# The context vector's adaLN products of a two-layer hybrid transformer, made by VectorE alone

## The chip, the cores and the metric

The kernel runs on one core of a Trainium2 chip. The metric is device time in microseconds (us), the median of the runs shown. The engines are TensorE (PE; its weight loads are PEld), VectorE (DVE), ScalarE (ACT), GpSimd (POOL) and SyncE (SP), which issues most loads. Each takes its own queue of instructions in order.

## The reference

Two layers work on a latent stream of 512 tokens and a context stream of 256 tokens, 1024 features each. Every sub-layer is normalised and modulated by shift, scale and gate vectors that come from a conditioning vector, one for the latent stream (`c`) and one for the context stream (`c_ctx`):

```python
silu_c = jax.nn.silu(c)
silu_cc = jax.nn.silu(c_ctx)
for layer in range(DEPTH):
    mod_l = (silu_c @ w_mod[layer] + b_mod[layer]).reshape(b, N_SUB, 3, 1, D_MODEL)
    mod_c = (silu_cc @ w_mod[layer] + b_mod[layer]).reshape(N_SUB, 3, D_MODEL)
    xl = macaron_ffn(xl, norm_g[layer, 0], mod_l[:, 0, 0], mod_l[:, 0, 1], mod_l[:, 0, 2], ...)
    xc = macaron_ffn(xc, norm_g[layer, 0], mod_c[0, 0], mod_c[0, 1], mod_c[0, 2], ...)
    # then a mixer (neighbourhood attention and Fourier mixing, or grouped attention
    # and spatial gating), and a second feed-forward with sub-layer 2's vectors
def modulate(h, shift, scale):
    return h * (1 + scale) + shift
def macaron_ffn(x, g, shift, scale, gate, w_gu, w_down):
    h = modulate(rms_norm(x, g), shift, scale)
    return x + 0.5 * gate * swiglu(h, w_gu, w_down)
```

`w_mod` is 1024 by 9216 for each layer. The last sub-layers need no context vectors, because only the latent stream is returned.

## The kernel before

Activations lie feature-major on the chip, eight tiles of 128 features by 768 tokens. Every float32 operand of a product is split in two float32r parts, high and low, and three products (L303 to L305) make one. The high part is a cast on ACT, the low part a subtraction on DVE (`fill`, L324 and L325, for weights; `finish`, L414 and L415, for activations).

The products with `w_mod` are not made by PE. A row block of 128 outputs by 512 or 1024 inputs is loaded with one output per partition, multiplied by silu(c) or silu(c_ctx), which lies repeated on every partition, and summed along the row. `mod_row` does this for each of the vectors in `vecs`: vector 0 is the latent one, vector 1 the context one. `mod_finish` adds the bias and prepares scale and gate.

Where the rows are made:

- `start_up` makes the vectors of the first sub-layer, rows of 1024, 24 of them for both vectors, k tile by k tile, between the first loads, the first norm and the first block products. `two_rows` gives each pair of rows one of three places in turn.
- `mod_jobs` makes jobs of half a row block, 512 columns. In `ffn`, `tick` adds a share to a counter after each group of products, and each time that it passes one, a job is traced. The first feed-forward has 96 jobs for both vectors, the second 80 for both, the third 64 for the latent vector alone, the fourth none. A job's weights go to `wm`, which has two buffers, by a load on SP's queue (L183); silu of the second half of the features replaces the first half's midway.

The order on the engines is set by a planner that simulates the program's times, within the dependencies. Besides those, `issue_after(ins)` puts what is traced inside behind `ins` on the engine of `ins`. `dve_last` is the newest of the DVE instructions that the block products wait for, and jobs pass it as `behind`. `pool_last` is the last POOL sum of `combos`, which makes four sums of blocks of the input.

Around the jobs, `gu_w` makes a tile of gate and up products by seven block products: seven weight blocks are formed by four POOL sums (L516 to L522) and split by ACT and DVE, ACT copies the first two results out of PSUM (L541, L544), DVE makes the sums of the others (L547, L551, L554, L555, L560), and ACT and DVE form the activations (L549 to L561). PE may write on in a bank only when ACT's copy of it is done.

Of the kernel before, what the change touches and what calls it, by code (L numbers as in the profile page):

```python
# [15 lines left out]
ALU = mybir.AluOpType  # L16
# [37 lines left out]
def hybrid_backbone_kernel(ctx: ExitStack, tc: tile.TileContext, A: dict, out: bass.AP):  # L54
# [9 lines left out]
    def opened(name, **kw):  # L64
        """a pool that is open from here until its second part is called"""
        es = ExitStack()
        return es.enter_context(tc.tile_pool(name=name, bufs=1, reuse_waits="tile", **kw)), es.close

    # PSUM: four banks, and four more that are single or in pairs as the phase wants them
# [20 lines left out]
    # ---------------------------------------------------------------- constants  # L90
# [13 lines left out]
    def load_constants(pool, l, shape):  # L104
        """per-head gains (those of the queries with the scores' factor, negated), head selectors and their transposes"""
        name = ("ab", "cd")[l]
        g = pool.tile([P, 2], F32, name="gq")
        nc.sync.dma_start(g, A["gqk_" + name])
        V.tensor_scalar(g[:, 0:1], g[:, 0:1], -HD ** -0.5, None, ALU.mult)
        res = [g]  # L110
        for a, sh in (("sel_", [P] + shape), ("bsel_", [32 + shape[1], shape[0], P])):
            o = pool.tile(sh, F32R, name=a + name)
            nc.gpsimd.dma_start(o, A[a + name])
            res.append(o)
        return res
# [4 lines left out]
    # ---------------------------------------------------------------- work that is emitted between groups of products  # L120
    pending = []
    down_last, act_last, pool_last = [], [], []
# [13 lines left out]
    # ---------------------------------------------------------------- adaLN vectors  # L136
    def load_silc(tiles, d0, n):
        """silu(c) and silu(c_ctx), n elements from d0, on every partition"""
        for v, t in enumerate(tiles):
            nc.sync.dma_start(t, A["cb"][:, v, d0:d0 + n])  # L140
            ACT.activation(t, t, AF.Silu)
        return tiles

    def mod_row(w, junk, silc, vecs, outs, behind=()):
        """products of 128 rows of weights with silc, an element of the vector per partition"""
        for v in vecs:
            if v == 1:
                with issue_after(pool_last):
                    POOL.tensor_tensor(w, w, silc[v], op=ALU.mult)  # L149
                ACT.activation(w, w, AF.Copy, accum_out=outs[v])  # L150
                continue
            with issue_after(behind):
                V.tensor_tensor_reduce(junk, w, silc[v], 1.0, 0.0, ALU.mult, ALU.add, outs[v])  # L153
# [16 lines left out]
    def mod_jobs(items):  # L170
        """items: (layer, sub, kind, vecs); a job takes 128 elements' products with a half of the features"""
# [23 lines left out]
    # ---------------------------------------------------------------- root mean square, inverse  # L195
# [4 lines left out]
    def rsqrt_sqrt(y, v, pool, shape, tag):  # L200
        """y = v ** -0.5; y and v: [p, n]: root, reciprocal and a Newton step"""
        t = pool.tile(shape, F32, tag=tag, name=tag)
        ACT.activation(y, v, AF.Sqrt)
        V.reciprocal(y, y)
        V.tensor_tensor(t, y, y, op=ALU.mult)
        V.tensor_tensor(t, t, v, op=ALU.mult)
        V.tensor_scalar(t, t, -0.5, 1.5, ALU.mult, ALU.add)
        V.tensor_tensor(y, y, t, op=ALU.mult)

    def rsqrt_newton(y, v, pool, shape, tag):  # L210
        """the same, v normal and above 0, without the root: a first guess by exponent, then three Newton steps"""
# [7 lines left out]
    class Norm:  # L219
        """RMSNorm and modulation of columns [c0, c0+n) of x into hh, hl"""  # L220
# [60 lines left out]
    # ---------------------------------------------------------------- weight blocks, split in two float32r parts  # L281
    def wsplit(pool, r, bufs, tag="w", eng=V):
        """[128, n] -> two float32r parts, n at most 1024"""
        n = r.shape[-1]
        h = pool.tile([P, n], F32R, tag=tag + "h", name="wh", bufs=bufs)
        lo = pool.tile([P, n], F32R, tag=tag + "l", name="wl", bufs=bufs)
        ACT.copy(h, r)
        eng.tensor_tensor(lo, r, h, op=ALU.subtract)
        return h, lo

    def wload(src, n=2048, parts=2):
        """one load of two blocks"""
# [4 lines left out]
    def by_k(w, k=KT):  # L297
        """split block [128, k * c] -> one (high, low) pair per k tile"""
# [8 lines left out]
    def issue_after(ins):  # L307
        """what is traced inside takes its turn on the engine behind ins"""
# [9 lines left out]
    # ---------------------------------------------------------------- half-step SwiGLU  # L318
    def fill(w, src, eng=V, behind=()):
        """a float32 block -> its two float32r parts"""  # L320
# [9 lines left out]
    def lead_ffn(fi):  # L330
        """the weights of the first three tiles, a part at a time; then where they are, and how to let go of them"""
# [10 lines left out]
    def lead_mixer(src, name):  # L342
        """the first blocks of an input projection, likewise"""
# [15 lines left out]
    def ffn(l, f, with_ctx, jobs=(), next_sub=None, opening=False, lead_in=None, lead_out=None):  # L359
        """Gate and up products of a tile are a 2 by 2 block product (gate / up, halves of the features,  # L360
        halves of the tokens). The first tiles take it as it stands, while the norms and the sums of blocks
        are being finished; the others take Winograd's seven block products."""
# [10 lines left out]
        with tc.tile_pool(name=f"ffn{fi}", bufs=1, reuse_waits="tile") as fp:  # L373
# [10 lines left out]
            def lead_slots():  # L384
                """[128, 512] pairs for the weights of the first three tiles, a pair per two k tiles"""
# [20 lines left out]
            def lead_k(w):  # L406
                """per k tile: gate and up"""
# [9 lines left out]
            def activate(act, c0, g, u):  # L417
                """of one stream's gate and up"""
# [10 lines left out]
            def gate_up(n):  # L429
                """places for a gate and an up product of n columns"""  # L430
# [22 lines left out]
            def lead(ws, each=None):  # L453
                """first tiles, k outermost, one stream after the other, while the norms are being finished"""
# [20 lines left out]
            def combos():  # L475
                """sums of blocks of the input: T1, T2, T3 and -T4"""
# [25 lines left out]
                for k in range(4):  # L502
# [6 lines left out]
                    pool_last[:] = [POOL.tensor_tensor(a, a, b21[1], op=ALU.add)]  # L509
# [143 lines left out]
    def start_up(tiles, slots, lead_k, fill, lead):  # L653
        """loads, first adaLN vectors, first norm and first tiles of the first sub-layer, k by k"""
# [14 lines left out]
        def two_rows(i):  # L669
            """room for two rows, in turn in three places"""  # L670
# [5 lines left out]
        def part(kt):  # L676
            """the vectors for a k tile and its weights"""
# [43 lines left out]
    # ---------------------------------------------------------------- pieces of the mixers  # L721
    FULL = slice(0, P)

    def head_rms(rooms, q, sel, width, rows, first, last):
        """sums of squares per head of one tile, a row per head; yields ahead of the products"""
# [12 lines left out]
    def rows_inverse(ap, nrow, nrow_c, e, rows, rr):  # L738
        """rows of sums -> rows of 1 / rms, in two float32r parts in rr"""
# [19 lines left out]
    def rows_tile(ap, nrow, **kw):  # L759
        """high parts of rows, low parts 32 partitions below, zeros between"""  # L760
# [17 lines left out]
    def weave(main, filler, share):  # L778
        """emit main; after each of its steps, enough of filler to have its share"""
# [52 lines left out]
    # ---------------------------------------------------------------- even layers  # L832
    def mixer_even(lead_in):
        xd = dram.tile([P, KT, T], F32, name="xd")
        if True:
# [7 lines left out]
            if True:  # L843
# [8 lines left out]
                # queries and keys of the first two pairs, latent columns first  # L852
# [24 lines left out]
                # the residual streams leave the chip until the output projection  # L877
# [6 lines left out]
                def qk_norm(t):  # L884
                    """yields between its parts; leaves qh, ql, kh, kl in qk[t]"""
# [37 lines left out]
                # values, token major  # L923
# [82 lines left out]
                def attention():  # L1006
                    # two heads of a tile of queries side by side; scores come negated
# [9 lines left out]
                    def keys(a, j):  # L1017
                        """key tiles of a unit, in the order of its scores"""
# [48 lines left out]
                    def stage_p(t, j):  # L1067
                        """values of both heads, feature major"""
# [48 lines left out]
    # ---------------------------------------------------------------- odd layers  # L1117
    def mixer_odd(lead_in):
        if True:
# [7 lines left out]
            if True:  # L1127
# [7 lines left out]
                # keys, values and queries, the first of them k outermost  # L1135
# [85 lines left out]
                def sgu(g, tails):  # L1221
# [16 lines left out]
                    # chunk, column group, (row, column)  # L1238
# [43 lines left out]
                def attention():  # L1282
                    # a head of either group of keys side by side; scores come negated
# [41 lines left out]
                    def stage_p(t, j):  # L1325
                        """values of both heads, feature major"""
# [43 lines left out]
    # ================================================================ layers  # L1370
# [26 lines left out]
def _layout(i):  # L1397
# [5 lines left out]
    def lat(a):  # [512, n] natural order -> column group, row, column in group  # L1403
        return a.reshape(8, 8, 8, -1).transpose(1, 0, 2, 3).reshape(512, -1)

    def blocks(w, n):  # [1024, n * m] -> [m, 128, 8 * n]
# [3 lines left out]
    def pairs(b):  # [2 * m, 128, n] -> [m, 128, 2 * n]  # L1410
# [10 lines left out]
    gu = i["ffn_w_gu"].reshape(4, 2, 4, 128, 2, 22, 128)  # f, half of k, k, p, gate or up, tile, m  # L1421
# [41 lines left out]
    # Fourier tables: channels (two groups of 64), latent positions in their order on chip, context positions  # L1463
# [15 lines left out]
    # odd layers: query heads t and t + 4 share a tile  # L1479
# [25 lines left out]
    trig = np.stack([np.cos(ang), np.sin(ang)], axis=1).astype(np.float32)  # [512, 2, 32]  # L1505
# [25 lines left out]
```

## Time and profile before

| | |
|---|---|
| runs | 2845.91, 2840.35, 2843.02 us |
| median of the runs | 2843.02 us |
| profiled execution, from its first to its last instruction | 2841.2 us |
| the median over this span | 1.8 us |
| granted PE clock, mean | 0.970 |
| busy: PE, DVE, ACT, POOL | 2648.6, 2188.0, 1213.8, 978.1 us |

The profile comes from one execution. Its own time is known by its span, so sums are made against the span, and the 1.8 us by which the median of the runs lies above it are added at the end. Busy time of an engine is time in which it had an instruction in work, waiting for a shared resource within an instruction included. Times in stretches are counted from the span's start.

### The profile page before, as it was taken

Reading aid. Unit: us, or ns where it says so; the run is one execution under the profiler, and the core shown is the slowest. Engines: PE = TensorE matmul, PEld = TensorE weight load, DVE = VectorE, ACT = ScalarE, POOL = GpSimd, SP = SyncE. Lnnn points to the kernel's source line nnn. Section 1 sums busy time; section 2 is a strip of 40 time slices with the busy share of each in tenths; the row PEclk is TensorE's granted clock in tenths of the full one; section 3 lists DMA queues with packets and bytes.
Section 4 is the critical chain, followed back from the end, with each engine's and each line's share of the span. In section 5 each row is a group of like instructions: output and inputs, shape, how many; then the busy total and the mean of one; then the engine's idle time right before and its main releaser. Section 6 shows DMA issues by size and latency. Waiting matters only on the chain.

```text
span 2841.2 us, 42081 instructions
## 1 busy us (share of the span) xinstructions
PE 2648.6 (93%) x15826; PEld 2393.1 (84%) x15826; DVE 2188.0 (77%) x3820; ACT 1213.8 (43%) x2512; POOL 978.1 (34%) x677
## 2 busy tenths in 40 slices
PE   3699999999999999899999988999999989999999
PEld 2589888987977788799899877999998767988988
DVE  8979889986466844998899877777777577577877
ACT  5334444444344542344444443333334455444443
POOL 4555545542121111555455323222212010143432
PEclk9899999999999999999999999999999999999999
DMA  6323333333111241133333321333323200303232
GB/s 236 106 75 117 123 110 123 112 114 117 63 55 48 67 158 38 49 123 113 121 112 108 99 83 53 107 104 108 115 97 104 81 31 1 119 35 108 93 108 90
DMA packets 81172, 271.69 MB, mean 96 GB/s; under 512 B 11002, under 2 KB 15518, under 8 KB 66248
## 3 DMA queue, kind: packets, MB, share of 16 engines
q1 hardware_dynamic: 80408, 268.76, 27.7%
q8 instruction: 124, 2.03, 0.3%
q14 instruction: 80, 0.66, 0.1%
q0 software_dynamic: 560, 0.24, 0.0%
HBM read 262.35 MB, written 5.24 MB: 94 GB/s over the span
## 4 chain that ended last, share of the span: by engine, by line
PE 62%; DVE 18%; ACT 4%; issue 3%; DMA 3%; POOL 2%; SPq 0%; DVEq 0%; ACTq 0%; POOLq 0%
PE ps L303 9%; PE ps L304 9%; PE ps L305 9%; PE pb L303 7%; PE pb L304 7%; PE pb L305 7%; DVE wl L325 5%; DVE junk L153 2%; PE pp L303 2%; PE pp L304 2%; PE pp L305 2%; PE ps L767 2%; ACT wh L324 2%; DVE xn L316 1%; DMA wm<-in_wmod 1%
## 5 line engine op out<-in xcount | busy, mean ns | idle before, releaser
L324 ACT CAST wh<-wr 128x512 fp32r<-128x512 f32 (+1 forms) x672 | 385.9, 590 | 571.6 <-PE pb L304 177.3
L325 DVE TENSOR_TENSOR wl<-wr,wh 128x512 fp32r<-128x512 f32 (+1 forms) x672 | 554.4, 837 | 93.7 <-ACT wh L324 88.8
L149 POOL TENSOR_TENSOR wm<-wm,silc 128x512 f32<-128x512 f32 x176 | 266.5, 1514 | 297.6 <-DVE mod L153 100.9
L303 PE MATMUL ps<-hh,wh 128*128 128x384 f32 (+2 forms) x728 | 252.1, 347 | 24.0 <-ACT u L541 18.9
L305 PE MATMUL ps<-hh,wl 128*128 128x384 f32 (+2 forms) x728 | 250.6, 344 | 2.2 <-DVE wl L325 1.2
L304 PE MATMUL ps<-hl,wh 128*128 128x384 f32 (+2 forms) x728 | 250.4, 344 | 0.0
L153 DVE CUSTOM_DVE_ANT_0 junk<-wm,silc 128x512 bf16<-128x512 f32 x240 | 225.2, 938 | 25.2 <-DMA wm<-in_wmod 20.1
L516 POOL TENSOR_TENSOR s<-wr 128x512 f32<-128x512 f32 x74 | 112.1, 1515 | 378.1 <-DMA wr<-in_wgs 245.8
L303 PE MATMUL pb<-hh,wh 128*128 128x384 f32 (+2 forms) x632 | 210.3, 333 | 29.6 <-ACT u L541 18.3
L304 PE MATMUL pb<-hl,wh 128*128 128x384 f32 (+2 forms) x632 | 209.4, 332 | 26.5 <-DVE hl L269 26.5
L303 PE MATMUL ps<-ah,wh 128*128 128x512 f32 (+1 forms) x640 | 218.9, 348 | 4.5 <-DVE u L560 3.7
L304 PE MATMUL ps<-al,wh 128*128 128x512 f32 (+1 forms) x640 | 220.7, 345 | 0.4 <-DVE al L415 0.4
L305 PE MATMUL ps<-ah,wl 128*128 128x512 f32 (+1 forms) x640 | 219.8, 344 | 0.0
L305 PE MATMUL pb<-hh,wl 128*128 128x384 f32 (+2 forms) x632 | 208.4, 330 | 0.2 <-DVE wl L325 0.2
L303 PE MATMUL pb<-tt,wh 128*128 128x384 f32 (+2 forms) x600 | 195.7, 326 | 13.5 <-ACT tt L481 13.5
L303 PE MATMUL pb<-ah,wh 128*128 128x512 f32 (+1 forms) x576 | 197.9, 354 | 7.6 <-DVE u L560 3.8
L304 PE MATMUL pb<-al,wh 128*128 128x512 f32 (+1 forms) x576 | 202.3, 351 | 2.5 <-DVE al L415 1.4
L304 PE MATMUL pb<-tt,wh 128*128 128x384 f32 (+2 forms) x600 | 196.4, 327 | 6.6 <-DVE tt L482 6.6
L305 PE MATMUL pb<-ah,wl 128*128 128x512 f32 (+1 forms) x576 | 200.8, 349 | 0.0
L305 PE MATMUL ps<-tt,wl 128*128 128x384 f32 (+1 forms) x600 | 195.6, 326 | 3.2 <-DVE wl L325 3.2
L303 PE MATMUL ps<-tt,wh 128*128 128x384 f32 (+1 forms) x600 | 195.3, 326 | 3.5 <-ACT wh L324 3.5
L305 PE MATMUL pb<-tt,wl 128*128 128x384 f32 (+2 forms) x600 | 195.8, 326 | 0.7 <-DVE wl L325 0.7
(373 smaller groups left out, 7379.1 us busy)
## 6 DMA issues: line engine op xcount, KB each, us to landing
wr<-in_wgs SPq DMA_DIRECT2D x76, 1024.0 KB
wm<-in_wmod SPq DMA_DIRECT2D x240, 256.0 KB
wr<-in_wdn SPq DMA_DIRECT2D x44, 768.0 KB
wr<-in_wdn SPq DMA_DIRECT2D x18, 512.0 KB
wr<-in_wgl SPq DMA_DIRECT2D x9, 1024.0 KB
wr<-in_wmod SPq DMA_DIRECT2D x16, 512.0 KB
wr<-in_wqk_ab SPq DMA_DIRECT2D x5, 1024.0 KB
bias<-in_bias_ab SPq DMA_DIRECT2D x12, 384.0 KB
```

What stands on the lines that cost most here:

```text
L149: POOL.tensor_tensor(w, w, silc[v], op=ALU.mult)
L153: V.tensor_tensor_reduce(junk, w, silc[v], 1.0, 0.0, ALU.mult, ALU.add, outs[v])
L303: PE.matmul(o, wh, rh, start=start, stop=False, skip_group_check=again)
L304: PE.matmul(o, wh, rl, start=False, stop=False, skip_group_check=again)
L305: return PE.matmul(o, wl, rh, start=False, stop=stop, skip_group_check=again)
L316: return V.scalar_tensor_tensor(xs, ps_ap, hgt[:, vec_index(c0), l * 3 + s, dt:dt + 1], xs, ALU.mult, ALU.add)
L324: ACT.copy(h[:, :n], src)
L325: eng.tensor_tensor(lo[:, :n], src, h[:, :n], op=ALU.subtract)
L516: POOL.tensor_tensor(f3, a11, a21, op=ALU.subtract)
L767: PE.transpose(out=o[:, c * P:(c + 1) * P], in_=p[:, c * P:(c + 1) * P], identity=ident)
```

## The change

In `mod_row` the context vector is treated as the latent one: one DVE instruction multiplies and adds up, where a POOL product, in place in the weights' tile, and an ACT copy with an accumulated sum stood. With that, `pool_last` has no reader and goes. The diff also takes comments and docstrings out, line for line, so that line numbers stay as they are until L146; those lines are left out here.

```diff
@@ -117,9 +117,9 @@
     pending = []
-    down_last, act_last, pool_last = [], [], []
+    down_last, act_last = [], []
@@ -133,22 +133,17 @@
     def mod_row(w, junk, silc, vecs, outs, behind=()):
...
         for v in vecs:
-            if v == 1:
-                with issue_after(pool_last):
-                    POOL.tensor_tensor(w, w, silc[v], op=ALU.mult)
-                ACT.activation(w, w, AF.Copy, accum_out=outs[v])
-                continue
             with issue_after(behind):
                 V.tensor_tensor_reduce(junk, w, silc[v], 1.0, 0.0, ALU.mult, ALU.add, outs[v])
@@ -506,7 +501,7 @@
                     POOL.tensor_tensor(a, b21[0], b, op=ALU.subtract)
-                    pool_last[:] = [POOL.tensor_tensor(a, a, b21[1], op=ALU.add)]
+                    POOL.tensor_tensor(a, a, b21[1], op=ALU.add)
                     dve_last[:] = [done(3, k, a)]
```

## Rows read from the trace of the kernel before

**Rows 1.** The page's first part: busy time, share of the span, instructions.

```profile
PE 2648.6 (93%) x15826; PEld 2393.1 (84%) x15826; DVE 2188.0 (77%) x3820; ACT 1213.8 (43%) x2512; POOL 978.1 (34%) x677
```

**Rows 2.** Stretches: PE, PEld, DVE, ACT, POOL busy (instructions); granted clock, DMA share, GB/s.

```profile
0.00:165.00 165.00, 97.67 (x461) 79.70 (x462) 138.94 (x214) 73.32 (x145) 86.60 (x51) 0.91 0.44 154
165.00:640.00 475.00, 446.06 (x2423) 419.28 (x2422) 425.57 (x678) 209.12 (x475) 252.75 (x172) 0.95 0.34 114
...
1200.00:1640.00 440.00, 420.80 (x2362) 400.27 (x2361) 387.08 (x613) 197.33 (x439) 215.27 (x144) 0.98 0.33 112
...
1760.00:2160.00 400.00, 397.53 (x2243) 379.13 (x2244) 302.48 (x545) 144.64 (x272) 98.68 (x72) 0.99 0.31 103
```

**Rows 3.** Stretches of 40 us within the first feed-forward, same columns.

```profile
320.00:360.00 40.00, 40.00 (x231) 37.26 (x230) 31.62 (x52) 15.30 (x35) 23.53 (x17) 1.00 0.34 116
360.00:400.00 40.00, 33.30 (x165) 32.39 (x164) 35.13 (x51) 19.02 (x44) 19.90 (x13) 0.87 0.33 112
...
440.00:480.00 40.00, 35.36 (x175) 33.82 (x174) 38.54 (x61) 20.07 (x46) 19.41 (x14) 0.87 0.36 119
```

**Rows 4.** Waits, 165 to 640 us: total us, times, longest.

```profile
PE ps L303 <- ACT u L541: 11.7, 6, 3.1
PE pb L303 <- ACT u L541: 9.1, 4, 3.6
...
SPq L183 <- ACT wm L150: 324.5, 85, 13.3
...
ACT wm L150 <- POOL wm L149: 110.8, 75, 5.7
```

**Rows 5.** Timeline around one stall: start, us, instruction, idle before it.

```profile
387.28 0.69 PE L303 MATMUL pb<-hh,wh 128*128 128x384 f32 x1 [3.57 <-ACT u L541]
...
386.15 0.63 ACT L150 ACTIVATE wm<-wm 128x512 f32<-128x512 f32 x1
...
383.57 1.61 DVE L556 TENSOR_TENSOR sg<-sg,u 128x384 f32<-128x384 f32 x1
...
383.12 1.65 POOL L149 TENSOR_TENSOR wm<-wm,silc 128x512 f32<-128x512 f32 x1 [0.63 <-DVE mod L153]
```

**Rows 6.** Instructions of L149 and L153, whole span: ns min/median/max, first and last start.

```profile
L149 POOL TENSOR_TENSOR wm<-wm,silc x176: 1262/1542/1853, 166.5 to 1613.4; 128x512 f32<-128x512 f32 x176
L149 POOL TENSOR_TENSOR wr<-wr,tt x16: 2331/2376/2878, 15.6 to 112.5; 128x1024 f32<-128x1024 f32 x16
...
L153 DVE CUSTOM_DVE_ANT_0 junk<-wm,silc x240: 672/683/1839, 165.7 to 2157.0; 128x512 bf16<-128x512 f32 x120
...
L153 DVE CUSTOM_DVE_ANT_0 tt<-wr,tt x16: 1208/1213/2597, 14.2 to 109.8; 128x1024 bf16<-128x1024 f32 x16
```

**Rows 7.** Stretches, L153 alone (product and read-out, so two each): DVE busy.

```profile
165.00:640.00 475.00, 95.94 (x192) 0.95 0.34 114
...
1200.00:1640.00 440.00, 75.17 (x152) 0.98 0.33 112
...
1760.00:2160.00 400.00, 47.36 (x118) 0.99 0.31 103
```

**Rows 8.** Stretches, L325 alone: DVE busy, then POOL busy.

```profile
165.00:640.00 475.00, 156.37 (x169) 0.00 (x0) 0.95 0.34 114
...
1200.00:1640.00 440.00, 157.88 (x172) 0.00 (x0) 0.98 0.33 112
...
1760.00:2160.00 400.00, 117.74 (x162) 0.00 (x0) 0.99 0.31 103
```

**Rows 9.** Timeline of the start-up, DVE and then POOL.

```profile
16.20 2.31 DVE L161 SCALAR_TENSOR_TENSOR gsc<-mod,ng 128x1 f32<-128x1 f32 x1
...
38.07 0.15 DVE L161 SCALAR_TENSOR_TENSOR gsc<-mod,ng 128x1 f32<-128x1 f32 x1
...
123.39 3.21 DVE L488 TENSOR_TENSOR tsum<-tsum,hl 128x384 f32<-128x384 f32 x2
...
15.61 2.88 POOL L149 TENSOR_TENSOR wr<-wr,tt 128x1024 f32<-128x1024 f32 x1 [14.20 <-ACT t L235]
```

## The prediction

> **What bounds the kernel now.** I began with the page's first part: TensorE (PE) is busy for 93% of the span, VectorE (DVE) for 77%, GpSimd (POOL) for 34% [rows 1]. A share over the whole span hides which stage loses time, so the next view was the table of stretches, cut at the stages where the edited function works [rows 2]. The reader should compare three lines. The stretch 165 to 640 us, called A here, is the first feed-forward; 1200 to 1640 us, called B, is the second; both carry jobs that make a latent and a context product. The stretch 1760 to 2160 us, called C, is the third feed-forward, whose jobs make a latent product only, so GpSimd makes no products in it. All three are made mostly of the same seven block products per tile. In C the PE is busy 397.5 of 400 us. In A it is 446 of 475 at a clock of 0.95, in B 421 of 440 at 0.98. The DVE is the other way round: 90% in A, 88% in B, 76% in C.
>
> What the lost PE time costs is seen in slices of 40 us. A slice without a stall takes 231 matmuls at full clock (2.4 GHz); the slice 360 to 400 takes 165, because PE is idle for 6.7 us and the granted clock then falls to a mean of 0.87, part of it at the lower level of 1.2 GHz [rows 3]. At 231 per 40 us, A's 2423 matmuls need 420 us and B's 2362 need 409 us. So A holds 55 us, and B 31 us, over what its matmuls need; C's 2243 need 388 and hold 12.
>
> The waits say who keeps PE idle: its first product of a group waits for ACT's copy at L541, 20.8 us in A [rows 4]. The copy is late because ACT takes its queue in order and stands at L150, waiting for the POOL product of L149, 110.8 us in A [rows 4]. One stall, in order of time [rows 5]: POOL's product runs from 383.12 for 1.65 us; the DVE product at L556 starts at 383.57 and takes 1.61 us, to 0.4 us after POOL's end, so that most of it is waiting; ACT's cast of that result follows, then L150 at 386.15, then the copy; PE starts at 387.28 after 3.57 us of nothing. Two things of the old form are in it: L149 has held up a DVE instruction, and L150 stands ahead of the copy.
>
> **The change part by part.** It removes 200 POOL products (176 of 512 columns, 24 of 1024) and 200 ACT accumulations with their read-outs, and adds 200 DVE fused products with read-outs, directly behind the 200 that are there. A product of 512 takes 1.54 us on POOL (median) and 0.683 us on DVE; one of 1024 takes 2.38 and 1.21 us (16 of the 24 are in the rows shown) [rows 6]. Loads, tiles and results stay. The ordering behind the POOL sums goes away and needs no price, since nothing is left that it orders; the comments cost nothing.
>
> What POOL's product costs the DVE is the heart of the sum. In the start-up, the same instruction on one column that needs 0.15 us elsewhere takes 2.31 us beside an L149 [rows 9]. I went through the DVE's timeline from 14 to 125 us: there are 24 pieces lengthened by over 1.4 us, as many as POOL products; the first and the last stand in [rows 9], and the excess over the unhindered times of the same instructions adds up to 47 us. So each costs the DVE some 1.96 us there. The SBUF page of the Trainium skill (State Buffer, section Who interferes with whom) says that a VectorE instruction with two SBUF inputs and a GpSimd instruction that reads SBUF exclude each other for the whole instruction; these rows agree. By that rule alone a POOL product of 1.26 us could hold the DVE by at most its length, 121 us for A's 96, and then A would run at PE's pace, which is the first rival below.
>
> *Start-up, 0 to 165 us.* DVE is busy 139 of 165 us and almost without a gap from 14 to 134 us. Removed: 47 us. Added: 24 x (1.21 + 0.08) = 31 us. Net 16 us less on the engine that paces this stage. Some of the last products lie beside the context norm, where PE and ACT also set the pace, so I take 12 us; the bounds are nothing and 16.
>
> *A.* Added: 96 products at what one costs in C, read-out included, 47.36 / 59 = 0.803 us, or 77 us [rows 7]. (At the unhindered 0.683 it would be 66; at A's own present price, 95.94 / 96, it would be 96.) Removed is the hold-up of the other DVE work, for which the trace gives two bounds. From below, two groups that can be compared directly: the old products fall from 0.999 to 0.803 (19 us for 96), and the splits of L325 from 0.925 to 0.727 (169 of them, 33 us) [rows 7, 8]; together 52 us, and DVE's sum becomes 425.6 + 77 - 52 = 450 us. From above, A as C with more products: 302.5 + (192 - 59) x 0.803 = 409 us [rows 2, 7]; this leaves out that A has two more directly multiplied tiles. I take the middle, 430 us: the unlisted groups with two SBUF inputs gain too, but part of A's surplus is those tiles. At 430 us the DVE is over PE's 420, so DVE is A's bound. The fullest slice of A's middle shows what it can reach: 38.5 of 40 us, or 96% [rows 3]. 430 / 0.96 = 448 us, 27 less than now. The bounds: 450 / 0.96 = 469 us, 6 less; and, as 409 / 0.96 = 426 is under what PE needs with C's 12 us added, 432 us, 43 less.
>
> *B.* The same working: added 76 x 0.803 = 61 us; listed relief 14 (products) + 33 (splits) = 47 us, so 387 + 61 - 47 = 401; as C, 302.5 + 93 x 0.803 = 377; middle 389, over 0.96 is 405 us, below the 409 that PE needs. PE paces B, with stalls: C, with DVE at 76%, holds 12 us over its need, B before, at 88%, 31. After, DVE would be at 92% but without ACT's wait. I take half of the 31, so 15 us less; the bounds are C's 12 over the need, 19 less, and all of the 31, nothing.
>
> *ACT, POOL and the loads.* ACT loses L150 (0.63 us in [rows 5], and a read-out) with its waits, POOL its 200 products; work is only taken away from both, so no cover is needed. Loads of the job's weights wait on SP for ACT's L150 for 324 us in A [rows 4]; two buffers are turned over, and now the DVE's second product frees them, sooner by POOL's and ACT's part. Weight loads queue behind them on SP, so they can only come earlier. The new wait is on the DVE itself: two products in a row hold what is behind them by 0.80 us more, which is mostly L325 (PE's low parts) and the sums L551 to L560 (PE's banks). In the stall told above, 0.80 would take the place of up to 1.2 us of hold-up and of ACT's 0.63.
>
> *Sum.* 12 + 27 + 15 = 54 us less than the profiled span: 2841.2 - 54 = 2787. The median of the runs is 1.8 us over that span, which I add: 2789 us.
>
> **The rivals.** *PE's pace everywhere.* If the hold-up removed is near the whole of each POOL product, A's and B's DVE work falls under PE's need and both run as C: 420 + 12 and 409 + 12 us, so 43 and 19 less, with 16 at the start 78 less: 2765 us. For it: C itself, and the start-up's 1.96 us. Against it: by the middle estimate DVE would be needed for 430 of A's 432 us.
>
> *DVE becomes the bound and the kernel slower.* Place: A first. The relief would have to be small, because POOL's remaining sums (L516 to L522, four per tile, all on the shared side) and the combos move into the room and go on holding up DVE instructions. A turns slower once DVE's sum passes 475 x 0.96 = 456 us, so once the relief is under 47 us, 0.49 us per product. At half of the listed relief: A 425.6 + 77 - 26 = 477, over 0.96 is 497 (22 more); B 425, over 0.96 is 443 (3 more); start-up 31 - 23 = 8 more; 33 in all, 2876 us. Against it: in C the same POOL sums leave products at 0.803. The page Perfetto Trace Analysis of the Trainium skill (section Optimizing Scalar/DVE Operations) advises the other direction, work off a saturated VectorE, and adds that a move between VectorE and GpSimd might not help because of the shared port; A's 90% makes this rival what that advice would give.
>
> *The wait only changes its name.* PE's stalls stay as long, now put down to DVE evacuations behind two products, and the start-up's gain is eaten by the context norm: 2836 to 2843 us. For it: A's DVE remains full. Against it: ACT's 110.8 us have no other cause.
>
> **How the numbers follow.** A measurement of this kernel can tell about 0.2%, 6 us, from no change. Chances: the forecast 0.54, PE's pace everywhere 0.22, the renamed wait 0.11 (0.07 of it within 0.2%, 0.04 just faster), the slower case 0.13. So faster 0.80, same 0.07, slower 0.13. The forecast's own range, with each of the three terms halfway to its bounds (66 to 30 us less), is 2777 to 2813. The range for the time reaches to 2756, under the first rival, and up to 2843, the renamed wait, and leaves out the slower case and little else.
>
> **What would show it.** In the profile after: no L149 or L150, twice the L153 with means near 0.80 us in A and B; DVE 425 to 435 us busy in A's work and a mean of L325 near 0.73 us; no PE wait for L541 beyond a few us; granted clock near 0.99 in both; job loads waiting for L153; the first block product some 12 us earlier. The prediction is wrong if L325 stays above 0.85 us, if PE waits for DVE rows for as long as it did for L541, or if the start-up grows.

## The result and the profile after

The changed kernel takes 2762.85 us (median of 4 runs), the kernel before 2844.28 us beside it: a ratio of 0.9713, 95% interval 0.9693 to 0.9734, so 2.9% faster. The forecast was 2789, the range 2756 to 2843, and the first rival, PE's pace everywhere, 2765. The profiled execution has a span of 2764.3 us.

Lines of the code are 5 lower behind `mod_row`: the products are L148, the splits L320, the bank copy L536. First the page's first part of the changed kernel, which answers to [rows 1]:

```profile
PE 2625.4 (95%) x15826; PEld 2375.3 (86%) x15826; DVE 2154.8 (78%) x4220; ACT 1078.0 (39%) x2112; POOL 662.8 (24%) x477
```

The DVE makes 200 products more (with their read-outs 400 instructions) and is busy for 33 us less than before, 2154.8 against 2188.0.

PE runs the same 15826 matmuls in all these kernels, so stages can be cut at the same matmul in each (the 462nd, 2883rd, 6337th and 8697th, which stand at 165, 640, 1200 and 1640 us in the kernel before). In the changed kernel the start-up ends at 139.4 us, A runs from there to 578.3, B from 1141.7 to 1554.8, C from 1679.2 to 2076.9. The stretches, as [rows 2]:

```profile
0.00:139.40 139.40, 90.71 (x462) 75.11 (x462) 125.15 (x261) 48.05 (x95) 28.24 (x27) 0.98 0.53 182
139.40:578.30 438.90, 431.32 (x2424) 408.05 (x2423) 414.05 (x871) 147.98 (x284) 114.78 (x77) 0.99 0.38 122
1141.70:1554.80 413.10, 412.67 (x2361) 394.99 (x2361) 370.53 (x749) 150.09 (x286) 101.09 (x68) 1.00 0.36 117
1679.20:2076.90 397.70, 397.16 (x2243) 379.18 (x2244) 301.38 (x542) 144.21 (x271) 98.63 (x71) 0.99 0.31 104
```

The start-up is 25.6 us shorter, A 36, B 27; C, cut at the same matmuls, is the same to 1 us. B is now all PE: 412.7 of 413.1 us at full clock. A is nearly so, with the DVE at 94%. The waits in A, as [rows 4]: PE's loss at the bank copy has gone from 20.8 to 4.0 us, and SP waits for the DVE's products instead of ACT:

```profile
PE ps L298 <- ACT u L536: 4.0, 3, 2.1
PE ps L298 <- DVE u L555: 2.7, 2, 1.4
...
SPq L178 <- DVE mod L148: 149.3, 47, 13.6
SPq L178 <- DVE mpart L148: 113.1, 38, 12.6
```

The stretches of A and B for the products alone, which answer to [rows 7]:

```profile
139.40:578.30 438.90, 156.27 (x384) 0.99 0.38 122
1141.70:1554.80 413.10, 118.93 (x288) 1.00 0.36 117
```

and for the splits alone, as [rows 8]:

```profile
139.40:578.30 438.90, 124.92 (x169) 0.00 (x0) 0.99 0.38 122
1141.70:1554.80 413.10, 124.42 (x172) 0.00 (x0) 1.00 0.36 117
```

A product with its read-out costs 156.27 / 192 = 0.814 us in A (0.999 before), a split 124.92 / 169 = 0.739 us (0.925 before).

### The profile page after: what moved, and what is told of

The parts are those of the page before. It is cut to its first block, busy times and chain, and to the rows that moved or that the text cites. A ratio compares the mean times of both kernels' runs of the same rounds, so it can differ in the third digit from the quotient of the medians.

```text
span 2764.3 us, 41711 instructions
## 1 busy us (share of the span) xinstructions
PE 2625.4 (95%) x15826; PEld 2375.3 (86%) x15826; DVE 2154.8 (78%) x4220; ACT 1078.0 (39%) x2112; POOL 662.8 (24%) x477
## 4 chain that ended last, share of the span: by engine, by line
PE 76%; DVE 16%; ACT 3%; issue 2%; DMA 2%; POOL 0%; SPq 0%; DVEq 0%; ACTq 0%; POOLq 0%
PE ps L298 11%; PE ps L299 11%; PE ps L300 11%; PE pb L298 10%; PE pb L299 10%; PE pb L300 9%; DVE wl L320 3%; PE pp L298 2%; PE pp L299 2%; PE pp L300 2%; PE ps L762 2%; DVE junk L148 2%; DVE xn L311 1%; PE ps L1073 1%; DVE tt L477 1%
## 5 line engine op out<-in xcount | busy, mean ns | idle before, releaser
L320 DVE TENSOR_TENSOR wl<-wr,wh 128x512 fp32r<-128x512 f32 (+1 forms) x672 | 494.7, 746 | 66.2 <-ACT wh L319 63.3
L148 DVE CUSTOM_DVE_ANT_0 junk<-wm,silc 128x512 bf16<-128x512 f32 x416 | 338.3, 813 | 6.7 <-ACT silc L141 3.8
L299 PE MATMUL ps<-tt,wh 128*128 128x384 f32 (+1 forms) x600 | 194.4, 324 | 0.0
L298 PE MATMUL ps<-tt,wh 128*128 128x384 f32 (+1 forms) x600 | 194.2, 324 | 0.0
```

Source lines behind the costliest of these rows:

```text
L298: PE.matmul(o, wh, rh, start=start, stop=False, skip_group_check=again)
L299: PE.matmul(o, wh, rl, start=False, stop=False, skip_group_check=again)
L320: eng.tensor_tensor(lo[:, :n], src, h[:, :n], op=ALU.subtract)
```

## The experiments

Theory L says that POOL's product shuts the DVE out while it runs, and that PE's stalls follow from the late DVE. Theory Q, its rival, says that ACT, standing at L150 in its queue, made PE's bank copy late. All times are medians; each kernel was timed against the kernel before on the same chip.

**The two halves.** `mod_row` keeps both forms, and either the jobs or the start-up ask for the old one:

```diff
         for v in vecs:
+            if v == 1 and old:
+                with issue_after(pool_last):
+                    POOL.tensor_tensor(w, w, silc[v], op=ALU.mult)
+                ACT.activation(w, w, AF.Copy, accum_out=outs[v])
+                continue
...
```

> Two theories of where the 81 us come from. L: the POOL product shuts VectorE's instructions with two SBUF inputs out while it runs. Q: ACT stands at its accumulation in its queue and PE's bank copy is late behind it. This kernel changes the 24 products of the start-up alone, the jobs' 176 stay on POOL and ACT. By the matmuls' times the start-up gained 25.6 us of the 77, so both theories expect 2844 - 25 = 2819 us if the stages are independent. If the start-up's gain is only the 16 us of VectorE work that I had counted, 2828.

> The other half: the 176 products of the jobs on VectorE, the 24 of the start-up as before. Both theories expect 2844 - 36 (first feed-forward) - 22 (second) = 2786 us, and the two halves together should add up to the whole; if they don't, the planner's order in one stage hangs on the other.

Measured: the start-up alone 2819.88 us (ratio 0.9911, 0.9893 to 0.9929), the jobs alone 2786.04 us (0.9796, 0.9777 to 0.9815). The halves add up: 0.9911 x 0.9796 = 0.971. The start-up is worth 25 us, not the 16 that I had counted, and neither half hangs on the other.

**ACT's accumulation without POOL's product.** In the jobs the context product is made by the DVE in place, and ACT sums it (the start-up passes None for `behind` and stays as changed):

```diff
+            if v == 1 and behind is not None:
+                with issue_after(behind):
+                    V.tensor_tensor(w, w, silc[v], op=ALU.mult)
+                ACT.activation(w, w, AF.Copy, accum_out=outs[v])
+                continue
...
```

> Jobs' context product by VectorE in place (tensor_tensor), its sum by ACT's accumulating copy as before; start-up as changed. No POOL product, so nothing to shut VectorE out, but ACT stands at the accumulation again, now for VectorE. L: as the changed kernel, 2763 to 2775 us, since VectorE's work is the same and ACT has 0.8 us more per product. Q: most of the 58 us of the two feed-forwards come back, 2800 to 2820 us, with PE waiting some 15 to 20 us for ACT's bank copy in the first.

Measured: 2768.29 us (0.9730, 0.9712 to 0.9748). Q fails. Its waits in A show ACT standing at the accumulation nearly as long as before the change, 92.9 us against 110.8, and PE's copy L541 on time all the same:

```profile
ACT wm L150 <- DVE wm L149: 92.9, 74, 5.4
...
PE ps L303 <- DVE u L560: 4.9, 1, 4.9
PE ps L303 <- ACT u L541: 3.8, 3, 2.3
```

A is 3.6 us longer than in the changed kernel, B 1.9; that is what the accumulations on ACT cost where POOL makes no product. What they cost beside POOL's products, when both are late at once, no run prices.

**POOL's product without ACT's accumulation.** The changed kernel, and POOL makes the job's product again into a tile that nobody reads:

```diff
                         mod_row(w, junk, state["silc"], vecs, outs, behind)
+                        if 1 in vecs:
+                            spare = fp.tile([P, 512], F32, tag="spare", name="spare", bufs=1)
+                            POOL.tensor_tensor(spare, w, state["silc"][1], op=ALU.mult)
```

> The changed kernel, and for each of the 176 jobs' context products also POOL's product of the same operands into a spare tile that nobody reads: POOL's work as before the change, ACT free. L: VectorE loses some 0.7 us per product on top of its own, in the first feed-forward 415 + 67 = 482 us of work, so the stage goes from 440 to some 500 us and the second from 416 to 445: 2763 + 90 = 2850 us, and the low-part splits go back from 0.74 to over 0.9 us. Q: no change, 2763 to 2770 us.

Measured: 2890.31 us (1.0169, 1.0143 to 1.0196): some 127 us over the changed kernel, for work whose result nobody uses. L had the direction, and was short by 40 us. Its A, first the whole stretch, then the splits and POOL's spare products alone:

```profile
141.20:654.30 513.10, 453.84 (x2423) 424.63 (x2422) 503.14 (x863) 146.92 (x283) 258.56 (x171) 0.93 0.32 103
141.20:654.30 513.10, 150.32 (x168) 0.00 (x0) 0.93 0.32 103
141.20:654.30 513.10, 143.06 (x94) 0.93 0.32 103
```

The DVE has the same instructions as in the changed kernel and is busy for 89 us more, 0.95 us per spare product (94 of them); 98% of the stage. A split takes 0.895 us again. Not every DVE instruction is held up. Two lines of this run (139 to 660 us), one instruction with one wide operand from PSUM and one from SBUF (L314, the residual), one with both from SBUF (L553), and under them the same two in the changed kernel (138.5 to 578.4 us):

```profile
L314 DVE SCALAR_TENSOR_TENSOR x<-pb,hgt,x 128x512 f32<-128x512 f32 (+1 forms) x55 | 36.1, 663 | 0.4 <-PE pb L303 0.3
...
L553 DVE TENSOR_TENSOR u<-u 128x384 f32<-128x384 f32 x17 | 20.7, 1219 | 0.1
```

```profile
L311 DVE SCALAR_TENSOR_TENSOR x<-pb,hgt,x 128x512 f32<-128x512 f32 (+1 forms) x55 | 36.2, 666 | 5.5 <-PE pb L300 5.4
...
L550 DVE TENSOR_TENSOR u<-u 128x384 f32<-128x384 f32 x17 | 9.4, 550 | 0.1
```

The one with one SBUF operand takes 0.66 us in both; the one with two, 1.22 us against 0.55. So a DVE that was merely fuller would not explain the longer splits. The waits in A of the run with the spare product:

```profile
PE ps L301 <- ACT u L539: 23.7, 7, 5.3
PE pb L301 <- ACT u L539: 17.9, 4, 6.9
...
ACT sg L550 <- DVE sg L549: 48.3, 16, 5.4
```

PE waits 41.6 us for ACT's bank copy, twice as long as in the kernel before, though ACT has no accumulation to make. ACT stands instead at instructions that wait for the DVE's rows, 48.3 us at the largest, where the changed kernel has 22.8:

```profile
ACT sg L547 <- DVE sg L546: 22.8, 17, 2.4
```

So a late copy on ACT does not need ACT's own added work: the row that named ACT named the last link.

**POOL work that reads nothing, and POOL work that holds no buffer.** Two controls, each in place of the spare product:

```diff
-                            POOL.tensor_tensor(spare, w, state["silc"][1], op=ALU.mult)
+                            for _ in range(2):
+                                POOL.memset(spare, 0.0)
```

```diff
-                            POOL.tensor_tensor(spare, w, state["silc"][1], op=ALU.mult)
+                            POOL.tensor_tensor(spare, state["silc"][0], state["silc"][1], op=ALU.mult)
```

> The changed kernel, and for each of the 176 jobs' context products two fills of a spare tile by POOL (memset, 128x512), which read nothing. POOL is busy beside VectorE, but has no SBUF input. If any POOL work slows VectorE, part of the 127 us that the spare product cost comes back in proportion to POOL's time, 2790 to 2850 us; if it takes an SBUF read on POOL, as the Trainium skill's page SBUF has it, 2763 to 2770 us.

> As the run with the spare POOL product, but the product reads the two silu tiles and not the job's weights, so it holds no buffer and waits for no load. L: the hold-up is the same, 2870 to 2900 us, unless the planner puts the products where VectorE has little to do. If the loss came from the weights' buffers being let go later, back to 2763 to 2780 us.

Measured: the fills 2761.38 us (0.9712, 0.9689 to 0.9736), the same as the changed kernel; the product of the silu tiles 2899.18 us (1.0197, 1.0172 to 1.0221). Neither waits for a job's load, so the planner put a large part of both in the start-up (189 of the 352 fills, which is the 216 POOL instructions below less the changed kernel's 27; 48 of the 176 products). That makes this stage the test, since the DVE is busy there almost without a gap. The start-up with the fills:

```profile
0.00:139.60 139.60, 90.85 (x461) 75.21 (x462) 125.13 (x265) 48.16 (x95) 124.21 (x216) 0.96 0.53 182
```

POOL is busy for 124 of 139.6 us, and the stage is as long as in the changed kernel, DVE's busy time the same (125.15 there). With products that read two tiles, the start-up and A, then those products alone:

```profile
0.00:187.10 187.10, 102.90 (x462) 82.22 (x463) 172.78 (x261) 47.77 (x95) 112.28 (x75) 0.89 0.39 136
187.10:664.60 477.50, 443.75 (x2424) 416.57 (x2422) 457.56 (x870) 146.73 (x284) 192.18 (x125) 0.96 0.35 112
...
0.00:187.10 187.10, 84.01 (x48) 0.89 0.39 136
187.10:664.60 477.50, 77.41 (x48) 0.96 0.35 112
```

48 products lengthen the start-up by 47.7 us, 0.99 us each, and 48 lengthen A by 38.6 us, 0.80 each (DVE's busy time there by 43.5). They hold no job's buffer, so the release of buffers isn't the cause. What the Trainium skill's page SBUF (State Buffer, section Who interferes with whom) says, that an instruction with two SBUF inputs on VectorE is shut out by a GpSimd instruction that reads SBUF and not by one that only writes, is what these two runs show, together with the two lines of the run before.

**What the DVE's products still cost.** Leave them out, or make them twice:

```diff
             with issue_after(behind):
+                if v == 1:
+                    V.tensor_copy(outs[1], outs[0])
+                else:
...
```

```diff
         for v in vecs:
+            for _ in range(2 if v == 1 else 1):
...
```

> The context products are left out: each is a copy of the latent element, one column (so the context stream is modulated by the latent vector). It shows what the 200 VectorE products still cost. If the feed-forwards run at PE's pace after the change, they go from 440 to 430 and from 416 to 414 us, and only the start-up, where VectorE is busy without a gap, gains some 25 us: 2725 to 2730 us. If VectorE is still the bound of the first feed-forward, that goes to 422 us: 2715 us.

> Every context product is made twice on VectorE. Added work: 31 us in the start-up, 77 in the first feed-forward, 60 in the second. VectorE would have 415 + 77 = 492 us of work in the first and 374 + 60 = 434 in the second, over 0.96 that is 512 and 452 us, so 72 and 36 us more, and 31 at the start: 2763 + 139 = 2902 us. If VectorE had room left in the first feed-forward, less than half of that.

Measured: without context products 2730.10 us (0.9603, 0.9579 to 0.9626), with two of each 2867.15 us (1.0081, 1.0052 to 1.0109). Without, in the start-up, A and B:

```profile
0.00:123.50 123.50, 89.80 (x462) 74.78 (x463) 98.30 (x240) 49.52 (x99) 27.79 (x27) 0.97 0.59 208
123.50:550.20 426.70, 425.51 (x2422) 403.60 (x2422) 356.33 (x773) 149.62 (x281) 111.24 (x76) 1.00 0.39 126
1109.60:1522.20 412.60, 412.45 (x2362) 395.09 (x2362) 322.56 (x671) 151.24 (x284) 96.18 (x68) 1.00 0.35 116
```

In B the products cost 0.5 us, so there they are hidden under PE; A still pays 12 us for them and the start-up 16. The time is at the end of what was expected for feed-forwards at PE's pace; the start-up gave 16 us and not the 25 of the expectation. Made twice, in the start-up, A, the mixer between, and B:

```profile
0.00:166.70 166.70, 98.75 (x462) 80.84 (x463) 153.17 (x311) 48.89 (x96) 27.65 (x27) 0.89 0.45 152
166.70:628.10 461.40, 437.96 (x2424) 412.01 (x2423) 454.33 (x961) 146.80 (x284) 115.11 (x76) 0.97 0.34 109
628.10:1235.00 606.90, 545.61 (x3456) 459.06 (x3454) 387.64 (x834) 234.08 (x450) 113.36 (x74) 0.94 0.22 75
1235.00:1668.40 433.40, 419.52 (x2361) 397.56 (x2361) 422.55 (x906) 148.56 (x286) 106.59 (x68) 0.99 0.34 113
```

My expectation was 35 us too high: in A the DVE fills up to 98%, and products that don't fit run on into the mixer, which is 43 us longer and has 62 of them. The start-up pays 27 us for 24 products. B is 20 us longer, with the DVE at 97%. So DVE is the edge on which the change stands: A had room for one product more per job, not for two.

**The theory carried on.** If each POOL product costs the DVE about a product, other POOL work should move too. First the block sums of `combos`, then also the four weight sums of `gu_w`, and beside the first the start-up's eight low parts:

```diff
-                    sums(POOL, b, b22, b12)
+                    sums(V, b, b22, b12)
...
-                    POOL.tensor_tensor(a, b21[0], b, op=ALU.subtract)
-                    POOL.tensor_tensor(a, a, b21[1], op=ALU.add)
+                    V.tensor_tensor(a, b21[0], b, op=ALU.subtract)
+                    V.tensor_tensor(a, a, b21[1], op=ALU.add)
```

```diff
-                POOL.tensor_tensor(f3, a11, a21, op=ALU.subtract)
-                POOL.tensor_tensor(a21, a21, a22, op=ALU.add)
+                V.tensor_tensor(f3, a11, a21, op=ALU.subtract)
+                V.tensor_tensor(a21, a21, a22, op=ALU.add)
...
-                POOL.tensor_tensor(a11, a21, a11, op=ALU.subtract)
+                V.tensor_tensor(a11, a21, a11, op=ALU.subtract)
...
-                POOL.tensor_tensor(a12, a12, a11, op=ALU.subtract)
+                V.tensor_tensor(a12, a12, a11, op=ALU.subtract)
```

```diff
-                fill([a[:, (kt % 2) * 256:(kt % 2) * 256 + 256] for a in slots[i][kt // 2]], ws[i], POOL if i == 0 else V)
+                fill([a[:, (kt % 2) * 256:(kt % 2) * 256 + 256] for a in slots[i][kt // 2]], ws[i], V)
```

> The changed kernel with the block sums of combos (L481 to L504, 20 POOL instructions of 384 or 256 columns per feed-forward) on VectorE too. L carried on: a POOL sum of 1.2 us shuts VectorE out for most of it where VectorE is waited for, and VectorE makes the same sum in 0.55 us. PE waits some 25 us for these sums in the second and third feed-forward; a third of that and 2 to 3 us in the others would go: 2750 us. If the two engines really share the work there, VectorE's chain gets 11 us longer in each and the time is 2775 us.

> As the last, and the four POOL sums of weight blocks per tile (L511 to L517) on VectorE as well, so that POOL has no work with an SBUF input in the feed-forwards. Per tile VectorE gets 4 x 0.68 = 2.7 us more and loses a hold-up of at most 4 x 0.8 = 3.2 us: in the first feed-forward, where VectorE is at 94%, no change to 10 us either way; in the last, where ACT's casts wait for POOL's sums, a few us less. 2735 to 2760 us if L is all that matters; 2780 us and more if a POOL sum costs VectorE less than the 0.68 us that it costs to make it there.

> As the first of these three, and the start-up's eight low parts that POOL makes (128x256, 1.1 us each) on VectorE (0.41 us). VectorE is busy without a gap there; each POOL instruction lengthens its neighbour by some 0.5 us, so 8 x (0.5 - 0.33) = 1 to 2 us less than the first of these three, within what can be told apart.

Measured: 2752.42 us (0.9673, 0.9654 to 0.9692), 2734.23 us (0.9608, 0.9590 to 0.9627) and 2754.05 us (0.9676, 0.9657 to 0.9695). The second is the fastest kernel that computes everything, 1.1% under the changed one (0.9608 / 0.9713). Its page, and its A:

```profile
PE 2609.4 (95%) x15826; PEld 2367.5 (87%) x15826; DVE 2155.6 (79%) x4596; ACT 1082.1 (40%) x2112; POOL 134.4 (5%) x101
```

```profile
139.00:566.20 427.20, 425.36 (x2424) 403.78 (x2423) 401.85 (x926) 149.23 (x285) 0.00 (x0) 1.00 0.39 125
```

The DVE makes 376 instructions more than in the changed kernel in the same busy time, 2155.6 against 2154.8 us, and POOL's 528 us of work are gone. A's DVE work even falls, from 414 to 402 us. The third's difference from the first can't be told from nothing, as expected. Of the second's gain over the changed kernel 12 us lie in A and 20 behind B (the table below), some 9 of these in the last feed-forward, which has no jobs (2015 matmuls in 304.0 us of the changed kernel, from 2460 us; 2012 in 295.0 here). PE's waits there, 6.3 us in all, are gone, and a weight sum takes 0.69 us on the DVE where POOL took 1.3 to 1.5. So a shorter sum may be a part of the gain; no run separates it from the relief of the DVE.

The stages of all kernels, in us between the starts of the same matmuls (the last column ends with the start of the last matmul):

| kernel | start-up | A | between | B | the rest |
|---|---|---|---|---|---|
| before | 165.0 | 475.1 | 560.1 | 439.8 | 1196.3 |
| changed | 139.4 | 438.9 | 563.4 | 413.1 | 1204.5 |
| start-up alone | 139.5 | 475.5 | 560.0 | 439.9 | 1198.6 |
| jobs alone | 165.4 | 437.3 | 561.6 | 414.3 | 1199.5 |
| ACT sums, no POOL product | 139.8 | 442.5 | 562.8 | 415.0 | 1198.6 |
| spare POOL product | 141.2 | 513.1 | 566.4 | 462.6 | 1198.8 |
| fills on POOL | 139.6 | 437.1 | 565.2 | 412.9 | 1199.4 |
| spare product of silu tiles | 187.1 | 477.5 | 583.3 | 443.0 | 1202.2 |
| no context products | 123.5 | 426.7 | 559.4 | 412.6 | 1198.3 |
| context products twice | 166.7 | 461.4 | 606.9 | 433.4 | 1198.7 |
| combos on DVE | 139.6 | 434.3 | 565.7 | 412.3 | 1197.8 |
| all sums on DVE | 139.0 | 427.2 | 563.7 | 413.0 | 1184.4 |
| combos and low parts on DVE | 137.6 | 433.0 | 561.0 | 412.5 | 1201.7 |

## Why the prediction was right, and where its sizes were not

The direction was right, and so was the mechanism that carries the sum, POOL's products holding up the DVE; what shows it is the spare product together with the fills and the ACT sums. All three terms were taken too small: 25.6 + 36 + 27 = 89 us against the forecast's 54; 11 of the 89 are given back elsewhere. That the time meets the first rival's 2765 to 2 us is in part luck: its A was 7 us too low, its B 8 too high, its start-up 10 too little, and it had no loss elsewhere.

*Start-up: 12 us forecast, 25.6 measured.* The term was mis-sized by counting all the added products against the pace. DVE's busy time fell by 14 us (139 to 125), near the 16 of the sum. But what PE waits for in the kernel before is the low parts of the latent norm, and after the change it hardly does. PE's waits in the start-up, before and after:

```profile
PE pb L304 <- DVE hl L269: 26.5, 9, 6.7
```

```profile
PE pb L299 <- DVE hl L264: 2.9, 4, 1.2
```

The DVE starts the last of these parts at 99.87 us before and at 79.35 after. The timelines of the kernel before and of the changed kernel:

```profile
99.87 2.83 DVE L269 SCALAR_TENSOR_TENSOR hl<-t,mod,hh 128x512 fp32r<-128x512 f32 x1
```

```profile
79.35 0.74 DVE L264 SCALAR_TENSOR_TENSOR hl<-t,mod,hh 128x512 fp32r<-128x512 f32 x1
```

Ahead of that point 18 of the 24 POOL products had run, worth 18 x 1.96 = 35 us, and only 14 of the 24 added ones have been made, 18 us; the other ten run later, beside PE's work on the context columns. The difference, 17 us, is most of the 20.5 by which it starts earlier; the nineteenth POOL product lies beside the part itself, whose 2.83 us against 0.74 add 2. Over the whole stage PE is idle for 18.6 us less (67.3 to 48.7) and busy for 7.0 less (97.7 to 90.7) on the same matmuls, at a granted clock of 0.98 instead of 0.91. That the 7 us are the clock's share alone was not tried by itself.

*A: 27 us forecast, 36 measured.* The price of a product was right (0.803 forecast, 0.814 measured), the split's too (0.727 and 0.739). What failed is "I take the middle, 430 us": DVE's work is 414 us, so PE, busy for 431 of 439 us, sets A's pace and not the DVE. Worked out as in the sum, the relief is 425.6 + 78 - 414 = 90 us, 0.93 per POOL product, where the middle stands for 73 and the listed groups for 52. Groups that I hadn't listed had been held up as well: `u<-u`, 0.55 us in the lines above, has a mean of 0.85 in the kernel before. The other bound, 409, came close, but in part by luck: it took C's 302 us as they are, though A has 2424 matmuls and C 2243. Without the products A's DVE work is 258 us and C's 254; the working gave no reason for that. The other figure, that DVE can be busy for 96% at most, was low; with the products doubled it is 98%. The rival's A of 432 was 7 us too low, since 12 us of the products still show.

*B: 15 us forecast, 27 measured.* "I take half of the 31" failed. DVE's work is 371 us, 90% of the stage, which I had thought enough for stalls; hardly anything of them is left, 413 us against the 409 that PE needs. Before, at 88%, there were 31 us of them. So a DVE at 90% does not by itself make them (with doubled products, at 97%, B is 20 us longer). That it is the time by which a single DVE instruction is late, as in the stall of [rows 5], fits, and was not tried by itself.

*Waits.* "ACT takes its queue in order and stands at L150" was given as one of two causes of PE's stalls. The run with ACT's sums shows that by itself it is worth 5 us of the 63 in A and B, and the spare product that PE waits for the same copy without it. Against the renamed wait I had put ACT's 110.8 us; they were the wrong thing to go by, since with ACT's sums 92.9 of them stay and PE's loss does not. Of the slower rival, the place was right for the spare product: A takes 513 us there, against 475 before. With doubled products A stays under that, at 461, and the time goes in the stretch behind it, 607 against 560. The relief, which had to be under 0.49 us per product, is 0.93 in A, and the products of silu tiles cost 0.8 to 1.0 us each. The advice of the Trainium skill's page Perfetto Trace Analysis (section Optimizing Scalar/DVE Operations), to work off a saturated VectorE, was the wrong way round here; its caution about the shared port is what the trace bears out, 2188.0 us of DVE time with POOL's products and 2154.8 without.

Some us stay open. Past A the changed kernel's profile gives back 11 us in the stretches between A and B and behind B, in the mixers and the feed-forward heads; kernels with the same code there differ by up to 6 us behind B as well, and I didn't try to tell a cause from the spread.

## What to carry to other kernels

Price a GpSimd instruction that reads SBUF by what it takes from VectorE too: beside a VectorE that works on two SBUF operands, having such work on GpSimd freed nothing here, and moving it to VectorE was free, 376 instructions in the same busy time. Of two stages alike in one trace, one held by stalls and one at PE's pace, the second is a bound of what a change can give the first; here it was closer than a sum over listed groups, which leaves out what isn't listed, but its work has to be scaled to the other stage's. And a wait's name is only its last link: ACT was named for PE's stalls in the kernel before and again in the run in which ACT had nothing to accumulate.

## What the runs showed of the hardware

A VectorE instruction on a single column, 0.15 us by itself, took 2.31 us while a GpSimd product of 2.88 us ran [rows 9]. VectorE instructions with two SBUF operands were lengthened so, those with one from PSUM were not (1.22 against 0.55 us, and 0.66 in both). POOL's fills, 0.525 us each, kept it busy for nine tenths of the start-up and lengthened nothing. The middle that I took for A stands for 0.76 us per product, half of its median of 1.54; where VectorE is busy almost without a gap, in the start-up, the price was 1.0 us for a product of 512 columns, whose shortest time is 1.26 us [rows 6].
